# A decoder layer's MLP: the sums of w_down formed later, h's first reload moved, and the last product and final norm taken tile by tile

## The chip, the cores and the metric

The kernel runs on one core of one Trainium2 chip. The metric is the time of one execution on the device in microseconds (us), lower is better. All data is float32 and starts and ends in DRAM.

## The reference

One layer of a hybrid decoder, on 1024 tokens of width 1024, cut here to its steps:

```python
h = x
n = rms_norm(h, ln_mix_g)
ya = dilated_mixture(rope(q), rope(k), v) @ w_branch_a      # 12 heads of 64
yb = stick_breaking(qb, kb, vb) @ w_branch_b                # 8 heads of 64
h = h + (sigmoid(ga + b) * ya + sigmoid(gb + b) * yb) @ w_out
h = h + memory_cross_attn(rms_norm(h, ln_x_g), rms_norm(mem, ln_mem_g), ...)
u = conv3(rms_norm(h, ln_ffn_g) @ w_up) + conv_b            # 1024 -> 2 x 2816
h = h + (silu(u[:, :2816]) * u[:, 2816:]) @ w_down          # 2816 -> 1024
out = rms_norm(h, ln_f_g)
```

## The kernel before, in words

Every product in full precision is three TensorE matmuls (`mm3`, lines 98 to 101): both operands are split into a high and a low part by ACT (L82) and DVE (L83), and high x high, low x high and high x low are summed in PSUM. A matmul has 128 x 128 weights and 512 columns.

The program goes through these stages: the dilated attention and then the stick-breaking attention (`sb_unit`), with the projections of later heads between their units; the merge of both branches under their gates; `w_out`; cross attention; then the MLP, in two parts.

**w_up** has 22 rows g of 128 features for the gate half (ug) and the value half (uv). The products follow a Strassen-like scheme with seven products of half size in place of eight, so a row has sums of weights (`sum_weights`, on DVE) and sums of results. Each row is three functions: `up_start` (loads of the weights, the first product into bank pA), `up_middle` (three products into pA and pB, and pD for rows from the tenth on) and `up_end` (two products, then convolution, silu and the product of the halves). The driver calls `up_start(g)`, `up_end(g - 1)`, `up_middle(g)`. `add_into` copies a PSUM bank into half of ug or uv by ACT and adds a sum to it by an accumulating DMA on POOL's queue (L918): uv<-U of U4 for the upper half, uv<-U of U2 for the lower half. Then `up_end` reads uv by ACT (L966) and twice by DVE (L967, L968). The results go to DRAM (`r_d`) by DMAs on POOL's queue. ug and uv share two buffers (tag "hu"), so a row's uv follows the uv of the row before in the same place.

The first ten rows (`NEARLY`) begin with results that were made early and are read back from `er_d` and `e_d`.

**w_down** (`down`) also has seven products, each over 11 pairs of rows kg and four tiles of 128 tokens. `run(ps, i, first, also)` loads product i's left operand from `r_d` and its right one from w_down or from `sd_d`, splits them (`dh`, `dl`) and goes over the four tiles for every kg; `also` is a list of DMAs, one issued after each kg from the fourth on, by which h is read back from `h_d`. `into` adds the banks to h and, where `last` is given, forms the squares for the final norm. `out_half` scales four tiles of h and stores them.

**The sums of w_down** in `sd_d` are made by DMAs alone (`weight_sums`, L515): for each of 11 pairs kg, four `put` of 256 KB, DRAM to DRAM on SP's queue (L519), and three accumulating `add` on POOL's queue (L522), of 512, 256 and 256 KB. They alternate and each waits for the one ahead. `sum_step` takes one step: block b starts at step 3b and does an operation every second step. Before, it is called once per unit of the stick-breaking attention (`p >= NA`) and once per step of the merge. Puts and adds are kept where the program wrote them by `keep_in_program_order`.

Elsewhere the order on every engine is set by the compiler's scheduler, which simulates a timeline and takes what it thinks ready; so instructions can stand in another order than written. PSUM banks come from `bank`, SBUF tiles from pools with a fixed number of buffers per tag; a tile waits until the last reader of its buffer is done.

Of the kernel before, what the change touches and what calls it, by code (L numbers as in the profile page):

```python
# [7 lines left out]
F32 = mybir.dt.float32  # L8
F32R = mybir.dt.float32r
# [33 lines left out]
def hybrid_layer(ctx: ExitStack, tc: tile.TileContext, x, xT, mem, memT, w_in, w_v, w_br, w_out, w_xq, w_xk, w_xv, w_xo, w_up,  # L43
# [492 lines left out]
    def sum_step():  # L536
        n = sums_n[0]
        sums_n[0] += 1
        for b, ops in enumerate(sums):
            d = n - 3 * b  # L540
            if 0 <= d < 12 and d % 2 == 0:
                ops[d // 2]()

    for fn in proj_pair(0):
        fn()
# [2 lines left out]
    for p in range(NA + NS):  # L548
        units = [(dil_step, (8 * p + i,)) if p < NA else (sb_unit, (p, i)) for i in range(8)]
        if p == NA:  # L550
            units[CPOS:CPOS] = [(combine, (0,)), (combine, (1,))]
            units = [(dil_step, (8 * NA + i,)) for i in range(3)] + units
        gemms = [(fn, ()) for fn in proj_pair(p + 1)] if p + 1 < NA + NS else []
        ng = len(gates) if p == NA + NS - 1 else GATES[p]
        for _ in range(ng):
            gemms.append((gate, (gates.pop(0),)))
        nu, ngm = len(units), len(gemms)
        if p == NA + NS - 1:
            ngm = TAIL_MIX
        k = 0  # L560
        for u, (fn, a) in enumerate(units):
            while k < ngm and k * nu <= u * ngm:
                gemms[k][0](*gemms[k][1])
                k += 1
            fn(*a)
            if p >= NA:
                sum_step()
        while k < len(gemms):
            gemms[k][0](*gemms[k][1])
            k += 1  # L570
# [64 lines left out]
        yT.append((hi, lo))  # L635
    merged = [act2(), act2()]
    for m in range(NK):
        sum_step()
        gs = []
        for j in (m, 8 + m):  # L640
            g = ap.tile([P, T], F32, tag="kg", name="g", bufs=4)
            nc.sync.dma_start(g, ga_d[j])
            nc.scalar.activation(g, g, AF.Sigmoid, bias=vec[:, V_BG + j:V_BG + j + 1])
            gs.append(g)
        ws = []
        for _, wh, wl in wchunks(w_br[m], 768):
            ws += [(wh[:, c:c + P], wl[:, c:c + P]) for c in range(0, wh.shape[1], P)]
        for th in range(2):
            hs = slice(th * HT, (th + 1) * HT)
            pa = pp.tile([P, HT], F32, tag="mm", name="pa", bufs=3)  # L650
            pbr = pp.tile([P, HT], F32, tag="mm", name="pbr", bufs=3)
            for j in range(6):
                yh, yl = yT[j]
                mm3(pa if j < 2 else pbr, ws[j], (yh[:, hs], yl[:, hs]), j in (0, 2), j in (1, 5))
            ga, gb = gs[0][:, hs], gs[1][:, hs]
            nc.vector.tensor_tensor(ga, pa, ga, op=ALU.mult)
            nc.vector.tensor_tensor(gb, pbr, gb, op=ALU.mult)
            nc.vector.tensor_tensor(ga, ga, gb, op=ALU.add)
            hilo(merged[th][0][:, m], merged[th][1][:, m], ga)
# [274 lines left out]
        return res  # L934

    def up_middle(g, u):
        for n in ("ug", "uv"):
            nc.gpsimd.memset(u[n][:, 0:2], 0.0)
        if g < NEARLY:
            nc.sync.dma_start(u["ug"][:, 2:2 + HT], e_d[g])  # L940
        else:
            d = bank("mm", 3, "pD")
            product(d, u["l12"], R["21"], True)
            add_into(u["ug"][:, 2:2 + HT], d, u["p1"])
        s1, s2, s3, u["s4"] = sum_weights(u)
        product(u["A"], s2, R["t2"], False)
        u["U2"] = etile("U2")
        nc.scalar.activation(u["U2"], u["A"], AF.Copy)
        u["B"] = bank("tr", 2, "pB")
        product(u["B"], s3, R["t3"], True)  # L950
        product(u["A"], s1, R["t1"], False)
        u4 = etile("U4")
        nc.scalar.activation(u4, u["A"], AF.Copy)  # L953
        add_into(u["uv"][:, 2 + HT:2 + T], u["B"], u4)

    def up_end(g, u):
        product(u["A"], u["s4"], R["22"], False)
        nc.scalar.activation(u["ug"][:, 2 + HT:2 + T], u["A"], AF.Copy)
        product(u["B"], u["l22"], R["t4"], False)
        add_into(u["uv"][:, 2:2 + HT], u["B"], u["U2"])  # L960
        ys = []
        for n, cw, cb, sign in (("ug", vec, V_CB + g, 0), ("uv", ncw, V_CB + NF + g, 1)):
            c0 = 3 * g if sign else V_CW + 3 * g
            x_ = u[n]
            y = htile([P, T], "hy", "y")
            nc.scalar.activation(y, x_[:, 2:2 + T], AF.Identity, scale=cw[:, c0 + 2:c0 + 3], bias=vec[:, cb:cb + 1])  # L966
            nc.vector.scalar_tensor_tensor(y, x_[:, 1:1 + T], cw[:, c0 + 1:c0 + 2], y, op0=ALU.mult, op1=ALU.add)  # L967
            nc.vector.scalar_tensor_tensor(y, x_[:, 0:T], cw[:, c0:c0 + 1], y, op0=ALU.mult, op1=ALU.add)  # L968
            if not sign:
                nc.scalar.activation(y, y, AF.Silu)  # L970
            ys.append(y)
        a = ys[1]
        nc.vector.tensor_tensor(a, ys[0], a, op=ALU.mult)
        kg = g // 2
        if g % 2 == 0:
            nc.gpsimd.dma_start(r_d[kg, 0], a[:, :HT])
            evens["a"] = a
            return
        (r11, r12), (r21, r22) = halves(evens["a"]), halves(a)
        nc.gpsimd.dma_start(r_d[kg, 1], r21)  # L980
        nc.gpsimd.dma_start(r_d[kg, 2], r22)
        t = [mp.tile([P, HT + 8], F32, tag="ts", name="ts", bufs=3)[:, :HT] for _ in range(4)]
        nc.vector.tensor_tensor(t[0], r11, r12, op=ALU.subtract)
        nc.gpsimd.dma_start(r_d[kg, 4], t[0])
        nc.vector.scalar_tensor_tensor(t[1], r22, -1.0, t[0], op0=ALU.mult, op1=ALU.subtract)
        nc.gpsimd.dma_start(r_d[kg, 5], t[1])
        nc.vector.tensor_tensor(t[2], r22, r12, op=ALU.subtract)
        nc.gpsimd.dma_start(r_d[kg, 6], t[2])
        nc.vector.scalar_tensor_tensor(t[3], t[1], -1.0, r21, op0=ALU.mult, op1=ALU.subtract)
        nc.gpsimd.dma_start(r_d[kg, 3], t[3])  # L990

    def down():
# [10 lines left out]
            hs = slice(ch * HT, (ch + 1) * HT)  # L1003
            return [lambda t=t: nc.sync.dma_start(h[t][:, hs], h_d[t][:, hs]) for t in range(4 * th, 4 * th + 4)]

        def run(ps, i, first, also=()):
            for kg in range(KG):
                if i == 1 and kg < 6:
                    where = (bp, "wr", 2), (bp, "wh", 2), (bp, "wl", 2)
                else:  # L1010
                    where = (dn, "rl", 6), *(((dn, "dh", 2), (dn, "dl", 2)) if kg % 2 else ((mp, "mh", 2), (mp, "ml", 2)))
                raw, hi, lo = (pool.tile([P, 2, HT], d, tag=tag, name=n_, bufs=b) for (pool, tag, b), n_, d in
                               zip(where, ("rl", "dh", "dl"), (F32, F32R, F32R)))
                nc.sync.dma_start(raw[:, 0], r_d[kg, i - 1])
                nc.sync.dma_start(raw[:, 1], left[i - 1](kg))
                split_to(hi, lo, raw)
                if kg >= 3 and kg - 3 < len(also):
                    tc.keep_in_program_order(also[kg - 3]())
                for t in range(4):
                    ts_ = slice(t * P, (t + 1) * P)  # L1020
                    mm3(ps[t], (hi[:, 0, ts_], lo[:, 0, ts_]), (hi[:, 1], lo[:, 1]), first and kg == 0, kg == KG - 1,
                        skip_group_check=True)

        def into(ps, th, ch, op, last=None):
            for t in range(4):
                hs = h[4 * th + t][:, ch * HT:(ch + 1) * HT]
                nc.vector.tensor_tensor(hs, hs, ps[t], op=op)
                if last is not None:
                    square(4 * th + t, ch, etile("sq"), last)

        def out_half(th):
            fo = bp.tile([P, 4, D], F32, tag="a2h", name="fo", bufs=2)
            for t in range(4 * th, 4 * th + 4):
                ft, rs = fo[:, t % 4], ssq[t][:, 1:2]
                nc.vector.tensor_tensor(ft, h[t], gF, op=ALU.mult)
                nc.vector.tensor_scalar(ft[:, 0:HT], ft[:, 0:HT], rs, None, op0=ALU.mult)
                nc.scalar.activation(ft[:, HT:], ft[:, HT:], AF.Copy, scale=rs)
                for c in (0, HT):
                    nc.sync.dma_start(out[t * P:(t + 1) * P, c:c + HT], ft[:, c:c + HT])

        run(A, 1, True, load_h(0, 0))
        into(A, 0, 0, ALU.add)
# [9 lines left out]
        into(A, 1, 1, ALU.subtract, 0)  # L1052
        run(B, 4, False)
        into(B, 0, 1, ALU.subtract, 1)
        out_half(0)
        run(A, 3, False)
        into(A, 1, 0, ALU.add, 1)
        out_half(1)

    mem_prep()  # L1060
    w_out_half(0)
# [118 lines left out]
```

## Time and profile before

| | |
|---|---|
| runs | 1784.14, 1780.95, 1777.82 us, median 1780.95 |
| profiled execution | 1780.45 us, span in the trace 1778.6 us, mean granted clock 0.986 |
| PE / DVE / ACT / POOL busy | 95% / 63% / 49% / 18% |
| DMA moved | 273.01 MB, mean 153 GB/s |
| chain that ended last | PE 66%, issue 13%, DMA 10%, DVE 5% |

Read it so: TensorE (PE) is the engine to fill; the others matter where PE waits for them. PE's busy time counts matmuls that run slowly as well, so the granted clock has to be looked at beside it. The stages in time: dilated attention to about 365 us, stick-breaking attention to 765, merge, w_out, cross attention and the early parts of w_up to about 1145, w_up's rows to 1548, w_down to 1765, and the end.

### The profile page before, as it was taken

What the parts mean: (1) busy time and instruction counts of PE and PEld (TensorE: products, weight loads), DVE (VectorE), ACT (ScalarE), POOL (GpSimd) and SP (SyncE); (2) the same over time, 40 slices, a digit from 0 to 9 for tenths busy, and PEclk for the clock granted to TensorE, in tenths of its full rate; (3) what the DMA queues carried; (4) which work ended last, traced back from release to release, by engine and by line L of the source; (5) the groups of instructions that cost most, each with busy time, mean ns of one, the idle gap of its engine ahead of it and who ended that gap; (6) DMA issues with size and microseconds to landing.
All of it is one profiled execution on the core that took longest, in us unless ns stands there. A gap on an engine that the chain in (4) does not pass through costs nothing.

```text
span 1778.6 us, 23614 instructions
## 1 busy us (share of the span) xinstructions
PE 1693.4 (95%) x8598; PEld 1378.1 (77%) x8598; DVE 1113.0 (63%) x1737; ACT 871.0 (49%) x1495; POOL 326.9 (18%) x511
## 2 busy tenths in 40 slices
PE   7999999998999899999999989798999999989997
PEld 5977777878878787788888767576778888778885
DVE  3764654468757466575645666777777767655556
ACT  5344544466345445444534455454555555534344
POOL 0442333221112110001000102222222222200002
PEclk9999999999999999999999999899999999999999
DMA  7443333455774843566322325666755454677664
GB/s 305 113 123 92 107 83 84 134 134 145 200 140 118 159 113 95 180 181 249 131 95 72 130 83 178 206 165 184 211 148 157 136 136 125 188 259 231 214 191 140
DMA packets 106388, 273.01 MB, mean 153 GB/s; under 512 B 16096, under 2 KB 16352, under 8 KB 106272
## 3 DMA queue, kind: packets, MB, share of 16 engines
q1 hardware_dynamic: 66368, 166.68, 28.9%
q0 software_dynamic: 39904, 104.82, 24.1%
q8 instruction: 68, 1.11, 0.3%
q14 instruction: 48, 0.39, 0.1%
HBM read 188.77 MB, written 74.29 MB: 148 GB/s over the span
## 4 chain that ended last, share of the span: by engine, by line
PE 66%; issue 13%; DMA 10%; DVE 5%; ACT 3%; POOL 3%; SPq 0%; POOLq 0%; DVEq 0%; ACTq 0%
PE mm L99 4%; PE mm L101 4%; PE mm L100 4%; PE pA L99 3%; PE pA L100 3%; PE pA L101 3%; DMA sd_d<-in_w_down_dram 2%; DMA uv<-U 2%; PE mmt L99 2%; PE dA L100 2%; PE dA L101 2%; PE mmt L100 2%; PE mmt L101 2%; PE dA L99 2%; DMA xw<-xs 2%
## 5 line engine op out<-in xcount | busy, mean ns | idle before, releaser
L101 PE MATMUL mm<-a2h,wl 128*128 128x512 f32 x592 | 235.2, 398 | 0.0
L99 PE MATMUL mm<-a2h,wh 128*128 128x512 f32 x592 | 234.7, 396 | 0.0
L100 PE MATMUL mm<-a2l,wh 128*128 128x512 f32 x592 | 234.5, 396 | 0.0
L83 DVE TENSOR_TENSOR wl<-wr,wh 128x1024 fp32r<-128x1024 f32 (+1 forms) x119 | 145.3, 1222 | 95.0 <-ACT wh L82 92.1
L82 ACT ACTIVATE wh<-wr 128x1024 fp32r<-128x1024 f32 (+1 forms) x119 | 124.0, 1043 | 132.6 <-PE mmt L101 29.2
L83 DVE TENSOR_TENSOR dl<-rl,dh 128x1024 fp32r<-128x1024 f32 x77 | 94.1, 1224 | 85.0 <-ACT dh L82 81.5
L82 ACT ACTIVATE dh<-rl 128x1024 fp32r<-128x1024 f32 x77 | 81.2, 1058 | 114.6 <-PE dA L101 41.2
L101 PEld LDWEIGHTS mm<-a2h,wl 128*128 128x128 f32 x592 | 112.4, 190 | 22.2 <-issue 1.0
L100 PEld LDWEIGHTS mm<-a2l,wh 128*128 128x128 f32 x592 | 112.3, 190 | 22.3 <-issue 0.9
L99 PEld LDWEIGHTS mm<-a2h,wh 128*128 128x128 f32 x592 | 112.5, 190 | 22.0 <-issue 0.9
L493 DVE TENSOR_TENSOR_SCAN kp<-kp 128x128 f32<-128x128 f32 (+7 forms) x64 | 86.8, 1356 | 29.4 <-ACT kp L490 29.1
L99 PE MATMUL pA<-a2h,mh 128*128 128x512 f32 x176 | 70.5, 400 | 14.9 <-ACT U L953 14.9
L502 ACT ACTIVATE at<-tra 128x512 f32<-128x512 f32 (+3 forms) x96 | 43.3, 489 | 76.9 <-PE tra L500 59.6
L112 POOL TENSOR_TENSOR ss<-ss,neghalf 128x1 f32<-128x1 f32 x24 | 23.3, 995 | 307.6 <-DVE ss L597 305.7
L490 ACT ACTIVATE kp<-zz,zsc 128x512 f32<-128x512 f32 (+3 forms) x96 | 55.6, 583 | 49.3 <-DVE zz L489 44.5
L381 ACT ACTIVATE sp<-sp,nm 128x128 f32<-128x128 f32 (+1 forms) x96 | 42.3, 442 | 72.6 <-DVE nm L379 72.5
L100 PE MATMUL dA<-dl,dh 128*128 128x512 f32 x176 | 70.1, 398 | 3.5 <-DVE dl L83 3.5
L101 PE MATMUL dA<-dh,dl 128*128 128x512 f32 x176 | 70.0, 397 | 0.0
L101 PE MATMUL pA<-a2h,ml 128*128 128x512 f32 x176 | 69.3, 394 | 0.0
L100 PE MATMUL pA<-a2l,mh 128*128 128x512 f32 x176 | 69.3, 394 | 0.0
L99 PE MATMUL dA<-dh 128*128 128x512 f32 x176 | 62.1, 393 | 3.8 <-ACT dh L82 3.8
L491 ACT ACTIVATE gg<-zz,zsc 128x512 f32<-128x512 f32 (+3 forms) x96 | 55.7, 583 | 7.1 <-DVE gg L494 7.1
(352 smaller groups left out, 4587.4 us busy)
## 6 DMA issues: line engine op xcount, KB each, us to landing
rl<-r_d SPq DMA_DIRECT2D x77, 256.0 KB, 3.2
wr<-in_w_in_dram SPq DMA_DIRECT2D x37, 512.0 KB, 4.2
wr<-in_w_up_dram SPq DMA_DIRECT2D x32, 512.0 KB, 4.3
w<-in_w_up_dram SPq DMA_DIRECT2D x22, 512.0 KB, 3.7
uv<-U POOLq DMA_DIRECT2D x44, 256.0 KB, 4.7
r_d<-ts POOLq DMA_DIRECT2D x44, 256.0 KB, 4.8
rl<-sd_d SPq DMA_DIRECT2D x44, 256.0 KB, 3.6
r_d<-y POOLq DMA_DIRECT2D x33, 256.0 KB, 3.4
```

The costliest lines, as they stand in the source:

```text
L82: nc.scalar.activation(hi, raw, AF.Copy)
L83: nc.vector.tensor_tensor(lo, raw, f(hi), op=ALU.subtract)
L99: nc.tensor.matmul(ps, wh, rh, start=first, stop=False, **kw)
L100: nc.tensor.matmul(ps, wh, ro, start=False, stop=False, **kw)
L101: nc.tensor.matmul(ps, wo, rh, start=False, stop=last, **kw)
L112: nc.gpsimd.tensor_tensor(ss, ss, neghalf[:, :n], op=ALU.pow)
L381: nc.scalar.activation(sp[:, a, :n], sp[:, a, :n], AF.Exp, scale=0.125, bias=nm[:, a:a + 1], accum_out=ost[:, 130 + a:131 + a])
L490: nc.scalar.activation(kp[:, c0:c1], z[:, :n], AF.Sigmoid, scale=zsc[:, 1, i:i + 1])
L491: nc.scalar.activation(gg[:, c0:c1], z[:, :n], AF.Sigmoid, scale=zsc[:, 0, i:i + 1])
L493: nc.vector.tensor_tensor_scan(rev, rev, rev, 1.0, op0=ALU.mult, op1=ALU.bypass)
L502: nc.scalar.activation(s[:, :nb * P], tp[:, :nb * P], AF.Copy)
```

## The change

`sum_step` is called in `up_middle` and `up_end` of w_up for rows g >= 6, and no longer in the attention and the merge. A block starts every second step and its six operations follow each other step by step. So there is one add in row 6, two in row 7, three in each of the rows 8 to 16, two in row 17 and one in row 18 (33), and 44 puts in the same rows. In `run`, the DMAs of `also` are issued from the seventh kg on in place of the fourth, and the loading and splitting is a function `operands`. With `ends=4`, which the last product has, the operands of the last four kg are loaded first and then taken tile by tile. `out_half` becomes `out_tile`, called by `into` after each tile of the last update of a half of h.

```diff
     def sum_step():
         n = sums_n[0]
         sums_n[0] += 1
         for b, ops in enumerate(sums):
-            d = n - 3 * b
-            if 0 <= d < 12 and d % 2 == 0:
-                ops[d // 2]()
+            d = n - 2 * b
+            if 0 <= d < 6:
+                ops[d]()
...
             fn(*a)
-            if p >= NA:
-                sum_step()
...
     for m in range(NK):
-        sum_step()
         gs = []
...
     def up_middle(g, u):
+        if g >= 6:
+            sum_step()
         for n in ("ug", "uv"):
...
     def up_end(g, u):
+        if g >= 6:
+            sum_step()
         product(u["A"], u["s4"], R["22"], False)
...
-        def run(ps, i, first, also=()):
-            for kg in range(KG):
...
-                nc.sync.dma_start(raw[:, 0], r_d[kg, i - 1])
-                nc.sync.dma_start(raw[:, 1], left[i - 1](kg))
-                split_to(hi, lo, raw)
-                if kg >= 3 and kg - 3 < len(also):
-                    tc.keep_in_program_order(also[kg - 3]())
-                for t in range(4):
-                    ts_ = slice(t * P, (t + 1) * P)
-                    mm3(ps[t], ...
+        def operands(i, kg):
...
+            nc.sync.dma_start(raw[:, 0], r_d[kg, i - 1])
+            nc.sync.dma_start(raw[:, 1], left[i - 1](kg))
+            return split_to(hi, lo, raw)
+
+        def run(ps, i, first, also=(), ends=0):
+            def step(t, kg, hi, lo):
+                ts_ = slice(t * P, (t + 1) * P)
+                mm3(ps[t], (hi[:, 0, ts_], lo[:, 0, ts_]), (hi[:, 1], lo[:, 1]), first and kg == 0, kg == KG - 1,
+                    skip_group_check=True)
+
+            for kg in range(KG - ends):
+                w = operands(i, kg)
+                if kg >= 6 and kg - 6 < len(also):
+                    tc.keep_in_program_order(also[kg - 6]())
                 for t in range(4):
+                    step(t, kg, *w)
+            ws = [(kg, *operands(i, kg)) for kg in range(KG - ends, KG)]
+            for t in range(4 if ends else 0):
+                for w in ws:
+                    step(t, *w)
...
                 if last is not None:
                     square(4 * th + t, ch, etile("sq"), last)
+                if last:
+                    out_tile(4 * th + t)
...
-        def out_half(th):
-            fo = bp.tile([P, 4, D], F32, tag="a2h", name="fo", bufs=2)
-            for t in range(4 * th, 4 * th + 4):
...
+        def out_tile(t):
+            if t % 4 == 0:
+                fo[t // 4] = bp.tile([P, 4, D], F32, tag="a2h", name="fo", bufs=2)
...
         run(B, 4, False)
         into(B, 0, 1, ALU.subtract, 1)
-        out_half(0)
-        run(A, 3, False)
+        run(A, 3, False, ends=4)
         into(A, 1, 0, ALU.add, 1)
-        out_half(1)
```

How the change moves instructions, at three places.

POOL's order in w_up, one row. Before, from the first instruction of row 13 to its second accumulate into uv (U is U4 in the first uv<-U and U2 in the second):

```order
L938 MEMSET ug 128x2
L938 MEMSET uv 128x2
L918 DMA ug<-p_11794 128x512
L976 DMA r_d<-y 128x512
L984 DMA r_d<-ts 128x512
L918 DMA uv<-U_11906 128x512
L918 DMA uv<-U_11879 128x512
```

Now, the same row from its uv on, with the first instructions of the next:

```order
L937 MEMSET uv 128x2
L915 DMA uv<-U_11876 128x512
L522 DMA sd_d<-in_w_down_dram 128x512 x2
L977 DMA r_d<-y 128x512
L522 DMA sd_d<-in_w_down_dram 128x1024
L985 DMA r_d<-ts 128x512
L915 DMA uv<-U_11849 128x512
L937 MEMSET ug 128x2
L915 DMA ug<-p_11903 128x512
```

The three adds of the sums (L522) and the two stores of `r_d` now stand between the two accumulates into the same uv.

SP's order in the same rows, loads of w_up's weights (`wr`, and `w` for the second half). Before:

```order
L901 DMA w_12067<-in_w_up_dram 128x1024
L72 DMA wr<-in_w_up_dram 128x1024
L901 DMA w_12206<-in_w_up_dram 128x1024
L72 DMA wr<-in_w_up_dram 128x1024
L901 DMA w_12358<-in_w_up_dram 128x1024
```

Now, with the puts of the sums (L519):

```order
L898 DMA w_12044<-in_w_up_dram 128x1024
L519 DMA sd_d<-sd_d 128x512
L519 DMA sd_d<-in_w_down_dram 128x512 x2
L72 DMA wr<-in_w_up_dram 128x1024
L898 DMA w_12190<-in_w_up_dram 128x1024
L519 DMA sd_d<-sd_d 128x512
L72 DMA wr<-in_w_up_dram 128x1024
```

Puts now stand between the loads of two rows' weights, and a put of the kind sd_d<-sd_d waits for an add.

PE at the end of the last product, its last twelve matmuls; dA_13129 to dA_13132 are the banks of the four token tiles, a dh its operands of one kg. Before:

```order
L99 MATMUL dA_13129<-dh_14701 128x512
L100 MATMUL dA_13129<-dl_14702,dh_14701 128x512
L101 MATMUL dA_13129<-dh_14701,dl_14702 128x512
L99 MATMUL dA_13130<-dh_14701 128x512
L100 MATMUL dA_13130<-dl_14702,dh_14701 128x512
L101 MATMUL dA_13130<-dh_14701,dl_14702 128x512
L99 MATMUL dA_13131<-dh_14701 128x512
L100 MATMUL dA_13131<-dl_14702,dh_14701 128x512
L101 MATMUL dA_13131<-dh_14701,dl_14702 128x512
L99 MATMUL dA_13132<-dh_14701 128x512
L100 MATMUL dA_13132<-dl_14702,dh_14701 128x512
L101 MATMUL dA_13132<-dh_14701,dl_14702 128x512
```

Now, the last two matmuls of the third tile and the first six behind them:

```order
L100 MATMUL dA_13131<-dl_14666,dh_14665 128x512
L101 MATMUL dA_13131<-dh_14665,dl_14666 128x512
L99 MATMUL dA_13132<-dh_14644 128x512
L100 MATMUL dA_13132<-dl_14645,dh_14644 128x512
L101 MATMUL dA_13132<-dh_14644,dl_14645 128x512
L99 MATMUL dA_13132<-dh_14651 128x512
L100 MATMUL dA_13132<-dl_14652,dh_14651 128x512
L101 MATMUL dA_13132<-dh_14651,dl_14652 128x512
```

Behind these stand six more of the same bank, of the operands 14658 and 14665, and nothing else; the other three tiles are done before.

## Rows read from the trace of the kernel before

**Rows 1.** The page's first part: busy time, share of the span, instructions.

```profile
PE 1693.4 (95%) x8598; PEld 1378.1 (77%) x8598; DVE 1113.0 (63%) x1737; ACT 871.0 (49%) x1495; POOL 326.9 (18%) x511
```

**Rows 2.** Busy time by stretch of the span.

```profile
core 0: us, PE busy (x) PEld busy (x) DVE busy (x) ACT busy (x) POOL busy (x), PEclk, DMA share, GB/s
200.00:320.00 120.00, 119.72 (x698) 95.33 (x698) 63.83 (x158) 59.55 (x157) 39.88 (x58) 1.00 0.35 91
365.00:765.00 400.00, 388.80 (x2299) 315.74 (x2298) 258.89 (x469) 195.11 (x352) 56.93 (x85) 0.99 0.61 146
492.00:507.00 15.00, 14.97 (x83) 11.13 (x82) 7.51 (x12) 6.85 (x13) 2.76 (x4) 1.00 0.93 159
615.20:620.00 4.80, 4.76 (x15) 3.85 (x16) 2.14 (x3) 3.30 (x7) 0.00 (x0) 0.50 1.02 136
1276.00:1465.00 189.00, 187.48 (x813) 152.63 (x814) 142.51 (x148) 103.24 (x134) 47.12 (x86) 1.00 0.54 148
```

**Rows 3.** What PE waited for: us in total, times, longest us.

```profile
PE pA L99 <- ACT U L953: 14.9, 8, 3.2
PE avs L507 <- ACT at L502: 7.6, 2, 5.0
PE dA L99 <- ACT dh L82: 3.8, 2, 2.1
PE dA L100 <- DVE dl L83: 3.5, 3, 1.6
```

**Rows 4.** Timeline near 608 us: start, length, instruction, [idle before, its releaser].

```profile
608.21 0.81 POOL L522 DMA_DIRECT2D sd_d<-in_w_down_dram  x1 [9.79 <-DMA sd_d<-sd_d]
609.30 0.84 POOL L513 DMA_DIRECT2D yt_d<-ye  x1
614.91 0.28 ACT L502 ACTIVATE at<-tra 128x128 f32<-128x128 f32 x1 [9.94 <-DMA yt_d<-ye]
615.24 0.69 PE L507 MATMUL avs<-at,v 128*64 128x128 f32 x2 [4.96 <-ACT at L502]
```

**Rows 5.** Timeline of one w_up row, uv's instructions.

```profile
1421.57 1.28 DVE L968 SCALAR_TENSOR_TENSOR y<-uv,ncw,y 128x1024 f32<-128x1024 f32 x1
1423.77 0.60 ACT L917 ACTIVATE uv<-pB 128x512 f32<-128x512 f32 x1 [0.54 <-PE pB L101]
1427.27 0.89 POOL L918 DMA_DIRECT2D uv<-U  x1 [1.49 <-ACT U L953]
1432.87 0.87 POOL L918 DMA_DIRECT2D uv<-U  x1 [4.71 <-ACT uv L917]
1437.24 1.24 ACT L966 ACTIVATE y<-uv,vec,ncw 128x1024 f32<-128x1024 f32 x1 [0.93 <-DMA uv<-U]
1446.62 0.89 POOL L918 DMA_DIRECT2D uv<-U  x1
```

**Rows 6.** DMA issues by window: KB each, median us to landing.

```profile
sd_d<-in_w_down_dram POOLq DMA_DIRECT2D x1, 512.0 KB, 11.7
sd_d<-in_w_down_dram POOLq DMA_DIRECT2D x1, 512.0 KB, 14.2
sd_d<-in_w_down_dram POOLq DMA_DIRECT2D x1, 256.0 KB, 5.2
ga_d<-xr POOLq DMA_DIRECT2D x1, 512.0 KB, 11.3
uv<-U POOLq DMA_DIRECT2D x20, 256.0 KB, 4.3
out_dram<-fo SPq DMA_DIRECT2D x1, 256.0 KB, 2.9
```

**Rows 7.** Timeline of the end.

```profile
1763.60 1.37 DVE L1027 TENSOR_TENSOR h<-h,dA 128x512 f32<-128x512 f32 x2 [6.55 <-PE dA L101]
1765.21 0.39 PE L101 MATMUL dA<-dh,dl 128*128 128x512 f32 x1
1769.36 5.72 SPq L1039 DMA_DIRECT2D out_dram<-fo  x8
```

More of the change, by code (lines that the diff above doesn't have):

```diff
@@ L1004, in load_h @@
             return [lambda t=t: nc.sync.dma_start(h[t][:, hs], h_d[t][:, hs]) for t in range(4 * th, 4 * th + 4)]
-        def run(ps, i, first, also=()):
-            for kg in range(KG):
[L1008 to L1013, printed above, removed]
-                nc.sync.dma_start(raw[:, 0], r_d[kg, i - 1])
-                nc.sync.dma_start(raw[:, 1], left[i - 1](kg))
-                split_to(hi, lo, raw)
-                if kg >= 3 and kg - 3 < len(also):
-                    tc.keep_in_program_order(also[kg - 3]())
-                for t in range(4):
-                    ts_ = slice(t * P, (t + 1) * P)
-                    mm3(ps[t], (hi[:, 0, ts_], lo[:, 0, ts_]), (hi[:, 1], lo[:, 1]), first and kg == 0, kg == KG - 1,
-                        skip_group_check=True)
+        def operands(i, kg):
+            if i == 1 and kg < 6:
+                where = (bp, "wr", 2), (bp, "wh", 2), (bp, "wl", 2)
+            else:
+                where = (dn, "rl", 6), *(((dn, "dh", 2), (dn, "dl", 2)) if kg % 2 else ((mp, "mh", 2), (mp, "ml", 2)))
+            raw, hi, lo = (pool.tile([P, 2, HT], d, tag=tag, name=n_, bufs=b) for (pool, tag, b), n_, d in
+                           zip(where, ("rl", "dh", "dl"), (F32, F32R, F32R)))
+            nc.sync.dma_start(raw[:, 0], r_d[kg, i - 1])
+            nc.sync.dma_start(raw[:, 1], left[i - 1](kg))
+            return split_to(hi, lo, raw)
@@ L1029, in into @@
                     square(4 * th + t, ch, etile("sq"), last)
-        def out_half(th):
-            fo = bp.tile([P, 4, D], F32, tag="a2h", name="fo", bufs=2)
-            for t in range(4 * th, 4 * th + 4):
[L1034 to L1039, printed above, removed]
+                if last:
+                    out_tile(4 * th + t)
+        fo = {}
+        def out_tile(t):
+            if t % 4 == 0:
+                fo[t // 4] = bp.tile([P, 4, D], F32, tag="a2h", name="fo", bufs=2)
+            ft, rs = fo[t // 4][:, t % 4], ssq[t][:, 1:2]
+            nc.vector.tensor_tensor(ft, h[t], gF, op=ALU.mult)
+            nc.vector.tensor_scalar(ft[:, 0:HT], ft[:, 0:HT], rs, None, op0=ALU.mult)
+            nc.scalar.activation(ft[:, HT:], ft[:, HT:], AF.Copy, scale=rs)
+            for c in (0, HT):
+                nc.sync.dma_start(out[t * P:(t + 1) * P, c:c + HT], ft[:, c:c + HT])
         run(A, 1, True, load_h(0, 0))
```

## The prediction

> **What bounds the kernel now.** Page first: TensorE (PE) is busy for 1693.4 of 1778.6 us, 95%, and no other engine passes 63% [rows 1]. So time is won only where PE idles or runs slowly, and lost wherever a new wait reaches PE. The busy time by stage comes next [rows 2]: in the w_up rows from the tenth on (1276 to 1465) PE is busy 187.48 of 189.00 us at full clock while the DMA engines are 54% used; in the stick-breaking stage, which now carries all the sums, they are 61% used, against 35% in the dilated stage before it, which has none. The list of what PE waited for [rows 3] is short: 7.6 us for `at` in the stick-breaking stage, 14.9 for `U` over eight first uses of a bank, and 3.8 and 3.5 at starts of products. The timeline then shows three places.
>
> Place 1, the worst stall of the stick-breaking stage [rows 4]. GpSimd (POOL) stood 9.79 us at an add of the sums, because that add reads what a put (sd_d<-sd_d) had not yet written. Behind it in POOL's order stood the store of `ye`; ACT's `at`, which takes over a buffer of the same tag, waited 9.94 us for that store, and PE 4.96 for `at`. For the next 4.80 us PE's granted clock was 0.50, 1.2 in place of 2.4 GHz [rows 2].
>
> Place 2, one steady row of w_up [rows 5]. A row's first accumulate into uv (of U4) is issued at 1427.27 and the next row's at 1446.62: a period of 19.35 us, equal to the row's PE work, so PE sets it. The second one (U2) goes out at 1432.87, 5.60 later, after POOL had waited 4.71 for ACT. `y<-uv` starts at 1437.24, released by its landing: 9.97 after the row's first issue. Then uv must be read by ACT (1.24) and twice by DVE (1.28 each), refilled by ACT (0.60), and `U` copied (0.60), before the next U4 can go: 5.0 us, 5.4 with 0.1 us for each of four handovers. So 9.97 + 5.4 = 15.4 of 19.35 are taken, and U2 may land 4.0 us later than now before the ring of uv becomes longer than PE's row.
>
> Place 3, the end [rows 7]. PE's last matmul starts at 1765.21; DVE takes up h at 1763.60; the stores go out from 1769.36 for 5.72 us and one needs 2.9 [rows 6].
>
> **The change, part by part.** Sums leave the attention stages: 33 adds and 44 puts are moved, none removed. Gain there: the 4.96 us stall goes, and with it the slow clock, 4.80 us at half speed = 2.4 us of work: 7.4 us. What would be late next at that place is `at` itself, whose other inputs PE had written before. PE's other wait of that line (7.6 - 5.0 = 2.6 us) I leave in. Bounds: 0, should the store of `ye` be late for the bank's sake anyway, and 10, if that other stall goes too (2.6). I take 7.4, since POOL's waiting ends on a put that is no longer there.
>
> The end: in the last four groups of the last product, three of the four token tiles now finish 12 matmuls or more before the end. At one matmul in 0.23 us (189 us for 813 in the w_up rows, [rows 2]) that is 2.8 us. Their h add, square, norm, scaling and stores then lie beside the last tile's matmuls; behind PE stays one tile's chain. Now 13.4 us lie between the start of the last matmul and the end of the span (1778.6 - 1765.21). I take 3 us of gain, the PE time handed over; bounds 1 (the chain of one tile with its store of 2.9 is not shorter) and 6 (the whole of the 5.72 us of stores shrinks to the last tile's).
>
> h reloaded three groups later: the same loads; at the first product PE waits 3.8 and 3.5 us for its own operands [rows 3], whose loads lie in front of h's. I put it at 0; bounds 4 gained (half of those 7.3), 1 lost.
>
> What w_up takes on: from the seventh row, one, two and then three adds a row (nine rows with three), and up to four puts of 256 KB on SP's queue between the loads of the weights. The order of POOL (shown above) has them between the U4 accumulate and the U2 accumulate of the same uv. The issue costs little: 0.5 to 0.9 us each, POOL idles. The landing matters, because what stands behind a batch in this queue lands behind it: such batches landed 11.7 and 14.2 us after the issue of the 512 KB add, and a plain store issued behind one needed 11.3 [rows 6]. A 256 KB add on its own took 5.2, the normal uv<-U 4.3. So in a row: U4 at 0, the three adds issued by 2.0, the last landed at 13.7 to 16.2, U2 some 2 us (about half of its 4.3) behind that: 15.7 to 18.2 instead of 9.97. With the 5.4 us of the ring the row becomes 21.1 to 23.6 us, 1.8 to 4.3 more than PE's 19.35. I take 3.0, the middle, for the eight rows from the tenth to the seventeenth: 24 us. For the rows with fewer adds (7, 8, 18 and 19) and the ninth, where the adds stand ahead of both accumulates, 2 us, bounds 0 and 8.
>
> A second count gives the same sign. Bytes: 0.54 x 19.35 = 10.4 us of a row are DMA time today. The sums cost (0.61 - 0.35) x 400 / 11 = 9.5 us of full DMA time a block [rows 2], an estimate, since the two stages differ in other transfers also. A block a row makes 19.9 of 19.35: the sixteen engines would be full. In the stretch 492 to 507, with a batch in flight, they were at 0.93. In a full queue every load of weights, every store and every accumulate is later. Bounds of the whole: 0, if all is absorbed, and 8 x 5.5 + 8 = 52.
>
> Sum: 1780.45 (the profiled execution) - 7.4 - 3 + 0 + 24 + 2 = 1796.05, **1796 us**. The profiled execution lies 0.5 us below the median of the runs shown, 1780.95; that is nothing against the terms.
>
> **Rivals.**
> *A, absorbed (faster).* The DMA engines have 46% to spare in these rows, POOL waits 4.71 us before U2 anyway, and U2 may land 4.0 us later at no cost. The batches measured above ran beside stores and loads of another stage. It decides at the last add of a batch: if it lands within about 12 us of U4's issue (13.97 less U2's 2), the row stays at 19.35. Then only the gains remain: 1780.45 - 7.4 - 3 = 1770. Against it: both batches seen took longer. The Trainium skill, "DMA: Bandwidth & Descriptors", section "Anatomy of one DMA — SWDGE (gpsimd) path", fits one transfer as 2.0 us plus its bytes over 436 GB/s; by that a row's three adds, one behind the other, would take an estimated 3.2 + 2.6 + 2.6 = 8.4 us and this rival would come true. The trace disagrees so far: 5.2 us for the small add alone, 11.7 and 14.2 for batches.
> *B, a draw.* Rows of about 20.5 to 20.9 us, 1.2 to 1.5 more: 8 x 1.35 = 10.8 eat the 10.4 that is gained: 1779 to 1783.
> *C, saturated (much slower).* SP holds puts that wait for adds, and the loads of weights queue behind those puts; the adds in turn wait for puts. The row then follows two full DMA trips and not one; at 25 us, 5.5 more, with 8 for the edge rows: 1780.45 - 10.4 + 52 = 1822. For it: at place 1 an add did stand 9.79 us for a put. Against it: SP is a step ahead of the row.
> *That the change does not do what it says:* the stall at 615 could stay, with the store of `ye` behind other POOL work. The forecast would be 7 higher, inside the range.
>
> **How the numbers follow.** About 0.3% (5.3 us) is what a measurement of this kernel tells from no change: faster is below 1775.6, slower above 1786.3. Rival A 0.29, since one favourable number (a batch some 3 us shorter) is enough. B 0.20: the lower end of my own row estimate (+1.8) lies near it. Slower 0.51: the forecast 0.38 (1787 to 1812 alone), C 0.13. The range takes in A with the larger gain at the end (1780.45 - 7.4 - 6 = 1767) and the upper bound of the cost with small gains (1780.45 - 5 - 1 + 52 = 1826).
>
> **What would show it.** In the changed profile: no POOL wait on sd_d and no 5 us stall near 615, so w_out begins some 7 us earlier; rows ten to seventeen at 21 to 24 us, with PE waiting for `uv` or `U` by way of uv<-U, whose landing is then 10 us or more (median 4.3 now); DMA share in these rows near 0.9; the span after the last matmul about 3 us shorter. If rows stay at 19.35 while uv<-U lands late, the ring was sized wrongly; if uv<-U lands in 5 us, the batches were, and A holds. If PE waits for weights (`mh`, `wh`) and not for uv, it is C.

## The result, and the profile after

The change is slower: median 1833.81 us (1829.25 to 1835.44, four runs) against 1779.65 (four runs of the kernel before beside them). The ratio is 1.0296, 95% interval 1.0269 to 1.0324, so 54 us were lost where the prediction had 16. Its sign was right, its size was not: the time lies outside the range, which ended at 1826.

Where the time went, by stage, from the two profiled executions (a stage ends at the first matmul of the next, a row of w_up at its first accumulate into uv; rows are counted from 1):

| us | before | after | difference |
|---|---|---|---|
| dilated attention, to the first stick-breaking matmul | 357.3 | 358.4 | +1.1 |
| stick-breaking attention | 381.2 | 376.1 | -5.1 |
| merge to the first matmul of w_up | 410.6 | 410.9 | +0.3 |
| w_up to row 1 | 11.8 | 11.9 | +0.1 |
| rows 1 to 8 | 134.4 | 144.5 | +10.1 |
| rows 9 to 17 | 171.4 | 220.3 | +48.9 |
| row 18 to the first matmul of w_down | 63.9 | 64.8 | +0.9 |
| w_down | 234.5 | 233.8 | -0.7 |
| after the last matmul's start | 13.4 | 11.8 | -1.6 |

The gains come to 7.4 us, and w_up lost eight times that (the rounded rows add up to 54.0, the spans differ by 53.8). The busy time by stretch of the change, rows 1 to 8, rows 9 to 17, and rows 10 to 17 alone (which took 154.5 us before):

```profile
1157.30:1301.70 144.40, 126.66 (x516) 100.38 (x515) 101.76 (x108) 72.46 (x91) 42.33 (x77) 0.95 0.76 204
1301.70:1522.00 220.30, 179.87 (x734) 143.31 (x734) 127.62 (x134) 93.28 (x121) 63.37 (x101) 0.92 0.87 195
1324.30:1522.00 197.70, 163.14 (x662) 129.87 (x663) 115.88 (x122) 85.00 (x111) 58.65 (x92) 0.91 0.89 194
```

PE no longer fills these rows as it does in [rows 2]. What it waits for in rows 9 to 17, and in the attention (`avs`), by the waits of the change:

```profile
PE pB L99 <- ACT uv L914: 36.7, 5, 9.0
PE pA L99 <- ACT U L947: 2.8, 1, 2.8
PE pA L99 <- ACT wh L82: 0.7, 1, 0.7
PE avs L507 <- ACT at L502: 4.0, 1, 4.0
```

The bank pB is not free until ACT has copied it to uv; weights (`wh`) cost it 0.7 us. With one more wait of 0.2 us, PE's waits in rows 9 to 17 come to 40.4 us. The other 8.4 of the 48.9 us lost there are PE's own matmuls: they kept it busy for 179.87 us, where the kernel before took 171.50 for about as many:

```profile
1295.30:1466.80 171.50, 171.50 (x747) 139.92 (x746) 127.69 (x133) 94.19 (x123) 42.91 (x79) 1.00 0.54 148
```

The granted clock was 0.92 in place of 1.00. The prediction counted a slow clock at place 1 and none here. What these rows would take with these waits at full clock no run shows.

In the chain that ended last, the accumulate has grown from 2% to 8%:

```profile
DMA uv<-U 8%; PE mm L99 5%; PE mm L101 5%; PE mm L100 5%; DMA xw<-xs 2%; PE mmt L99 2%; PE mmt L100 2%; PE dA L100 2%; PE dA L101 2%; PE mmt L101 2%; PE pA L99 2%; PE dA L99 2%; PE pA L100 2%; PE pA L101 2%; PE dB L101 2%
```

Row 15 of the change in its timeline, to be read against [rows 5]:

```profile
1448.33 0.92 POOL L915 DMA_DIRECT2D uv<-U  x1
1448.89 2.89 POOL L522 DMA_DIRECT2D sd_d<-in_w_down_dram  x3
1450.51 1.85 POOL L991 DMA_DIRECT2D r_d<-ts  x1
1451.92 1.33 POOL L915 DMA_DIRECT2D uv<-U  x1
1468.95 1.24 ACT L967 ACTIVATE y<-uv,vec,ncw 128x1024 f32<-128x1024 f32 x1 [9.80 <-DMA uv<-U]
1470.28 1.28 DVE L968 SCALAR_TENSOR_TENSOR y<-uv,ncw,y 128x1024 f32<-128x1024 f32 x1 [12.71 <-ACT y L967]
1473.00 0.60 ACT L914 ACTIVATE uv<-pB 128x512 f32<-128x512 f32 x1 [2.81 <-DVE y L969]
1473.65 0.79 PE L99 MATMUL pB<-t4h,wh 128*128 128x512 f32 x1 [8.79 <-ACT uv L914]
1474.38 0.86 POOL L915 DMA_DIRECT2D uv<-U  x1 [1.20 <-ACT U L952]
```

U2's accumulate is issued at 1451.92, earlier in its row than in [rows 5] (3.6 against 5.6 us), yet `y<-uv` is released by its landing only at 1468.95, after ACT idled 9.80 and DVE 12.71 us. From there on the order is as before: two passes of DVE, ACT's copy, PE (8.79 us idle, then 0.79 us for a matmul in place of 0.40), the next row. The row took 26.1 us. All rows with three adds between the accumulates, by the issue and the landing of their DMAs in the trace, each in us from the row's first accumulate:

```
row            10    11    12    13    14    15    16    17   mean
last add    +14.0 +18.3 +11.1 +16.5 +14.0 +17.4 +11.3 +17.2   15.0
U2 lands    +18.3 +19.6 +13.5 +20.1 +16.6 +20.5 +13.7 +20.6   17.9
next row    +27.7 +25.1 +21.3 +25.6 +24.4 +26.1 +21.6 +26.1   24.7
before:
U2 lands    +11.3 +13.8  +9.7  +9.6 +11.0  +8.7  +9.9 +11.3   10.7
next row    +18.1 +20.0 +19.2 +19.0 +20.5 +18.2 +19.3 +20.1   19.3
```

Landing by landing, U2 comes 1.3 to 4.3 us behind the last add, and the next row follows U2 by 5.5 to 9.4 us.

### The profile page after: what moved, and what is told of

Same layout as the page of the kernel before. It is cut to its first block, busy times and chain, and to the rows that moved or that the text cites. A ratio compares the mean times of both kernels' runs of the same rounds, so it can differ in the third digit from the quotient of the medians.

```text
span 1832.4 us, 23607 instructions
## 1 busy us (share of the span) xinstructions
PE 1712.1 (93%) x8598; PEld 1391.5 (76%) x8598; DVE 1116.1 (61%) x1737; ACT 870.2 (47%) x1495; POOL 325.3 (18%) x511
## 4 chain that ended last, share of the span: by engine, by line
PE 62%; DMA 13%; issue 10%; DVE 7%; ACT 5%; POOL 3%; SPq 0%; POOLq 0%; DVEq 0%; ACTq 0%
DMA uv<-U 8%; PE mm L99 5%; PE mm L101 5%; PE mm L100 5%; DMA xw<-xs 2%; PE mmt L99 2%; PE mmt L100 2%; PE dA L100 2%; PE dA L101 2%; PE mmt L101 2%; PE pA L99 2%; PE dA L99 2%; PE pA L100 2%; PE pA L101 2%; PE dB L101 2%
## 5 line engine op out<-in xcount | busy, mean ns | idle before, releaser
L100 PE MATMUL mm<-a2l,wh 128*128 128x512 f32 x592 | 234.5, 396 | 0.0
L99 PE MATMUL pA<-a2h,mh 128*128 128x512 f32 x176 | 72.1, 410 | 20.5 <-ACT U L952 17.7
L968 DVE SCALAR_TENSOR_TENSOR y<-uv,ncw,y 128x1024 f32<-128x1024 f32 x22 | 28.2, 1284 | 96.9 <-ACT y L967 96.9
L99 PE MATMUL pB<-t4h,wh 128*128 128x512 f32 x88 | 39.8, 452 | 36.7 <-ACT uv L914 36.7
```

The source lines that it names most:

```text
L99: nc.tensor.matmul(ps, wh, rh, start=first, stop=False, **kw)
L100: nc.tensor.matmul(ps, wh, ro, start=False, stop=False, **kw)
```

## The experiments

Three theories stand against each other. **Q** (queue): U2's accumulate lands behind the adds that POOL issued before it, and the ring of uv waits. **D** (demand): the sums fill the sixteen DMA engines wherever they stand. **S** (the prediction's rival C) says that puts on SP's queue hold up the weights. Ratios are to the kernel before, run beside each on the same chip; they carry 95% intervals.

**1. The sums back in the attention; the other two edits stay.** `sum_step` is called where it was.

> The change without its first part: the sums are made in the attention and the merge, as before; the later reload of h and the tile-by-tile end stay. Theory (the loss is all in w_up): w_up is back at 381.6 us, the stall of 5.0 us near 615 is back, the end is 1.6 shorter and w_down 0.7 shorter, as in the trace of the change: about 1777.5 us, ratio to before 0.998 to 0.9995. Rival (the end or the reload costs something that the slow w_up hides): 1782 or more.

Measured: 1779.71 us, 0.9978 (0.9963 to 0.9993). w_up is 382.1 us, `avs` waits 8.5 us again (longest 5.4), the end takes 11.8. The loss is all in the moved sums.

**2. Only the sums moved.**

> Only the sums are moved. Theory: first product of w_up 3.8 us earlier, w_up 59.9 us longer, as in the trace of the change: 1779.65 - 3.8 + 59.9 = 1835.7 us. Rival (part of the loss comes from the other two parts): under 1825.

Measured: 1832.42 us, 1.0285 (1.0259 to 1.0311); w_up 440.6 us. As expected.

**3. Same sums, same rows, behind U2.**

```diff
     def up_end(g, u):
-        if g >= 6:
-            sum_step()
...
         add_into(u["uv"][:, 2:2 + HT], u["B"], u["U2"])
+        if g >= 6:
+            sum_step()
+            sum_step()
```

(and none in `up_middle`).

> The whole change, with both steps of the sums of a row called in up_end behind the accumulate of U2, so that POOL's order has the adds behind both accumulates into uv; same bytes in the same rows. Theory Q (queue: U2's accumulate lands behind the adds, and the ring of uv waits for it): uv<-U lands again about 10 us after the row's first issue, rows of 19.4 to 20.5 us, total 1775 to 1790 us. Rival D (the sixteen DMA engines are full, wherever the adds stand): rows stay at 23 to 26 us, total 1820 or more.

Measured: 1786.61 us, 1.0021 (1.0006 to 1.0036): nine tenths of the loss is gone with the same bytes in the same rows. Rows 9 to 17 take 182.9 us in place of 220.3. Rows 1 to 8 take 139.1 in place of 144.5; there PE's order is another as well, see run 5. Rows 10 to 17 of that run:

```profile
1315.20:1478.00 162.80, 156.84 (x675) 125.83 (x674) 115.60 (x122) 84.83 (x113) 58.71 (x95) 1.00 1.02 237
```

What is left of PE's wait for uv in rows 9 to 17:

```profile
PE pB L99 <- ACT uv L914: 3.3, 2, 2.7
```

And the accumulates in its DMA issues, with the median landing, some still late behind other traffic:

```profile
uv<-U POOLq DMA_DIRECT2D x17, 256.0 KB, 8.2
```

Here the DMA share is 1.02 at 237 GB/s, against 0.89 at 194 in the change. So D is no bound on the change. It is the likely reason for what is left, 162.8 us for eight rows, 20.4 a row and 1.0 over the 19.3 before; run 6 bears on it.

**4. Puts alone.** The adds are not issued, so the sums are not formed; the puts stay.

> The whole change with the 33 adds of the sums left out; the 44 puts stay on SP's queue (the sums are then not formed). Theory Q: rows of w_up back at 19.3 us, total 1833.8 - 59.9 + 1 = 1775 us. Rival S (puts between the loads of the weights make w_up late): rows over 21 us, total over 1795. Rival D (bytes): the puts are about two fifths of what the sums move, so some 24 us of the 59.9 stay: 1798.

Measured: 1785.02 us, 1.0015 (0.9997 to 1.0032). Rows 9 to 17 fall to 175.1 us, 3.7 over before. But the puts have no add to wait for here and go out sooner: 24 of the 44 in rows 1 to 8, where the change has 9. Rows 10 to 13 still have four puts each, as in the change, and take 79.4 us against 76.3 before and 99.6 in the change, so puts by themselves are out. Puts that wait for adds can't occur in this run; for them the waits of the change speak. SP's queue stood 153.0 us for adds there:

```profile
SPq L519 <- DMA sd_d<-in_w_down_dram: 153.0, 21, 24.3
```

Yet PE waited only 0.7 and 0.2 us for weights in rows 9 to 17. So S is out in the change.

The ratio is 1.0015 where theory Q's 1775 us would be 0.9974, and the reason stands in rows 1 to 8: 145.8 us with no add anywhere. The 24 puts may have a part in that; but rows 3 to 5 of the change, which have two puts and no add, took 55.3 us against 50.0 before. Something else had slowed them.

**5. t4 ahead of t2 again.** In rows 4 to 9 the scheduler of the change had moved the product pB<-t4 of a row behind pA<-t2 of the next. The two accumulates of row 4 in the timeline of the kernel before:

```profile
1209.80 0.88 POOL L918 DMA_DIRECT2D uv<-U  x1 [0.45 <-ACT uv L917]
1214.59 0.89 POOL L918 DMA_DIRECT2D uv<-U  x1 [1.98 <-DVE y L967]
```

And of the change:

```profile
1209.16 0.88 POOL L915 DMA_DIRECT2D uv<-U  x1 [0.72 <-ACT uv L914]
1218.09 0.88 POOL L915 DMA_DIRECT2D uv<-U  x1 [2.10 <-ACT uv L914]
```

U2 goes out 8.9 us into the row in place of 4.8, behind twelve more matmuls of 0.23 us and a copy. It lands at 12.3 us in place of 10.4, and the row takes 18.3 in place of 17.0. The edit pins the first matmul of t2, for 0 < g < 10, behind what PE was given before it:

```diff
-        nc.tensor.matmul(ps, wh, rh, start=first, stop=False, **kw)
+        m = nc.tensor.matmul(ps, wh, rh, start=first, stop=False, **kw)
+        if pin:
+            tc.keep_in_program_order(m)
...
-        product(u["A"], s2, R["t2"], False)
+        product(u["A"], s2, R["t2"], False, 0 < g < NEARLY)
```

> The whole change, with the product t2 of rows 2 to 10 pinned behind product t4 of the row before on PE, the order that the kernel before had there. Theory O (order): from the fourth row on the scheduler of the change put t4 behind t2, U2's accumulate goes out 3 to 4 us later in a row and the ring of uv takes 18 to 19 us where PE needs 17; pinned, the first nine rows (first accumulate of row 1 to that of row 9) take about 136 us in place of 144.4, total 1826, ratio to before about 1.025. Rival (those 10 us come from the first adds and their traffic): 143 us or more, total 1832 or more, ratio 1.029.

Measured: 1830.03 us, 1.0266 (1.0246 to 1.0286), and 140.9 us for the eight rows. Half a hit: of the 10 us some 3.6 are gone. Run 3, whose PE order in these rows is that of before, has 139.1, so the order is worth about 4 to 5 us. Most of it shows in rows 3 to 5, ahead of the first add: 55.3 us in the change, 51.7 here and 51.0 in run 3. What is left, about 5 us, is not split further. The pin also moved the swap on: from row 12 the scheduler now puts t4 behind the next row's t2, and rows 9 to 17 took 224.0 us.

**6. Spread and behind U2.** Run 3 with the pin of run 5, and a block of the sums every third step over rows 1 to 21.

> The change with the adds behind U2's accumulate, t4 pinned ahead of t2, and the sums spread over rows 1 to 21 (a block every third step, an operation every second: one or two adds a row in place of three). Theory Q with D as the rest of the cost (three adds a row fill the DMA engines, DMA share 1.02 with the adds behind U2 and 1.3 us a row lost): DMA share about 0.8, w_up 382 to 386 us, the attention 5 us shorter as in the change, the end 1.6 shorter: ratio to before 0.995 to 0.998. Rival (anything in POOL's queue in w_up delays the stores and reads of these rows): w_up over 390, ratio over 1.001.

Measured: 1780.01 us, 0.9988 (0.9974 to 1.0001). Rows 9 to 17 take 172.5 us, 1.1 over before: with fewer adds a row, behind U2, the cost there is gone. But rows 1 to 8 take 143.4 and w_up 391.7, so the rival holds for the first rows, whose DMA share rose to 0.89 from 0.65 before. The ratio lies between what the two said.

**7. Thin, but between the accumulates.** The change's places, with the same slower steps over rows 1 to 20.

> The change with the adds where it has them, between the two accumulates into uv, but with a block of the sums every third step and an operation every second step, over rows 1 to 20: one or two adds a row in place of three. Theory Q says that a row pays only when U2's accumulate lands more than 4 us later than before: with one or two adds it lands at about 8 to 13 us after the row's first issue, and from the ninth row's first accumulate to the eighteenth's it takes 171 to 185 us; the earlier rows pay for order and traffic as in the change: ratio to before 1.000 to 1.012. Rival (a cost for each add, 48.9 us for 30 adds): the same 33 adds cost the same 50 us, ratio 1.025 or more.

Measured: 1804.18 us, 1.0109 (1.0087 to 1.0131); rows 9 to 17 took 182.4 us, as theory Q had it. That is not in proportion to the adds: 18 of them in these rows cost 11.0 us, where the change's 24 cost 48.9. A threshold is seen row by row: of its rows 9 to 17, those where U2 landed 8.6 to 13.3 us after the first issue took 17.3 to 18.6 us; where it landed at 13.9 to 17.1 they took 19.7 to 22.8. Rows 1 to 8, with adds from the start, took 157.8 us, which the expectation did not price.

**8. U2 by DVE.** The whole change, and one line:

```diff
-        add_into(u["uv"][:, 2:2 + HT], u["B"], u["U2"])
+        nc.vector.tensor_tensor(u["uv"][:, 2:2 + HT], u["B"], u["U2"], op=ALU.add)
```

> The whole change, with U2 added to the lower half of uv by DVE straight from PSUM, in place of ACT's copy and POOL's accumulating DMA: nothing that y reads then lands behind the adds of a row, while the sums move the same bytes in the same rows; 256 KB of accumulate a row are gone. Theory Q: rows 10 to 17 take 19.3 to 20.5 us in place of 24.7, total 1775 to 1790 us, ratio to before 0.996 to 1.005. Rival D (DMA engines full): 23 us or more a row, ratio over 1.015.

Measured: 1786.13 us, 1.0040 (1.0018 to 1.0061). Most rows from the tenth on take 19.3 to 21.3 us with all sums in the change's places; two take 25.2 and 27.5. Rows 1 to 8 fall to 131.5. The edit also removes 256 KB of accumulate a row, which run 3 did not. In the two long rows PE waits for something new, the weights that S had named:

```profile
PE pD L99 <- ACT wh L82: 11.2, 3, 6.1
```

So with U2 out of the queue the next limit shows, at DMA share 0.94 (from 1312 to 1478 us), and it is worth about 14 us.

**9. The store of `ye` by ACT.** Run 1 with `nc.scalar.dma_start` in place of POOL's for yt_d.

> Sums where the kernel before has them, the new end and the later reload, and the store of ye (yt_d) issued by ACT and not by POOL, so that no add of the sums stands ahead of it. Theory: the stall of 5 us near 615 and its slow clock go without moving the sums: 5.5 us less than the run with the sums back, ratio to before about 0.995. Rival (ACT now waits for DVE's copy, or at waits for something else): ratio 0.998 or more.

Measured: 1776.53 us, 0.9966 (0.9949 to 0.9982). The time is near the expectation and its reason isn't: the stick-breaking attention took 385.8 us, no less than before. The stall at 615 is gone, and others are there, by that run's waits from 358 to 744 us:

```profile
PE tra L500 <- DVE gg L494: 4.7, 4, 3.8
PE avs L507 <- ACT at L502: 4.1, 2, 3.9
```

Its profile has the gain in rows 1 to 8 (129.4 us), which the edit does not touch. How much of this is the spread between executions stays open: the same stage, with the same order on PE, took 131.8 to 134.4 us in four other profiles.

**10. The tile-by-tile end alone.**

> Only the tile-by-tile end; sums and h's reload as before. Theory: the end after the last matmul 1.6 us shorter, the rest the same: ratio to before 0.998 to 0.9995. Rival (the later reload of h carries the gain of the run with the sums back, 0.9978): ratio 0.9995 to 1.001.

Measured: 1781.87 us, 0.9994 (0.9982 to 1.0006): the end is 11.8 us in its profile in place of 13.4, too little to be told from no change by time.

**11. The sums between the attention and w_up.** Run 1 with `sum_step` in the merge, w_out, the keys and queries of the cross attention and its softmax.

> The new end and the later reload, and the sums made between the attention and w_up: one step of them per step of the merge, of w_out, of the keys of the cross attention, of its queries and of its softmax, a block every third step. There the DMA engines are 25 to 61% used and nothing on POOL's queue is awaited by a ring. Theory: the attention is 5 to 6 us shorter as in the change, w_up is 378 to 382 us as before, the end 1.6 shorter: ratio to before 0.994 to 0.997. Rival (the puts on SP's queue hold up the loads of w_out's weights, whose splits PE waits for): the stages between are 5 us or more longer, ratio 0.998 or more.

Measured: 1826.19 us, 1.0231 (1.0203 to 1.0260), a clear miss. The stages between took 463.0 us in place of 410.6; the steps followed each other faster there than in the attention, and 60 of the 77 transfers went out between 800 and 980 us. That stretch:

```profile
800.00:980.00 180.00, 152.83 (x682) 123.97 (x681) 76.97 (x127) 61.95 (x102) 30.94 (x43) 0.91 0.87 216
```

And PE's longest waits from 736 to 1000 us:

```profile
PE pv L99 <- ACT wh L82: 14.9, 3, 6.5
PE mmt L99 <- ACT wh L82: 5.5, 2, 3.1
```

And the wait of SP's queue for adds in the whole of that run:

```profile
SPq L519 <- DMA sd_d<-in_w_down_dram: 83.5, 19, 9.4
```

Here the rival fits, the loads of weights on SP's queue behind puts that wait for adds. It is not all: PE's waits for weights in these stages are 24.2 us (1.1 before) of the 52.4 lost, and PE's busy time grew by 18.2 at a granted clock of 0.94 (0.98 before).

**12. The sums back, and U2 by DVE.** Run 1 with the line of run 8: the sums in the attention, the new end, the later reload, U2 by DVE.

> A version that may beat both: the sums where the kernel before has them, the new end and the later reload, and U2 added by DVE. Theory: in rows 1 to 9 the kernel before is also held by the ring of uv (U2 lands 10 to 12 us after the row's first issue and the next row begins 5 to 6.6 behind that, 16.8 us for about 16.4 us of matmuls); with DVE the first nine rows take about 128 in place of 134 us, the later ones 19.0: ratio to before 0.994 to 0.997. Rival (DVE, which is 75% busy in these rows, is late with its splits): ratio 0.998 or more.

Measured: 1768.42 us, 0.9938 (0.9919 to 0.9957), faster than both kernels. Rows 1 to 8 take 126.9 us (134.4 before); rows 9 to 17 take 171.5, as before, since PE sets them. Rows 1 to 8 (a stretch of 128 us about them) and rows 10 to 17:

```profile
1162.00:1290.00 128.00, 118.16 (x505) 93.95 (x504) 106.83 (x120) 67.78 (x82) 32.88 (x68) 1.00 0.63 184
1304.70:1459.40 154.70, 154.70 (x673) 126.11 (x672) 118.84 (x128) 82.24 (x104) 31.16 (x60) 1.00 0.44 130
```

The rival is out: DVE carries the additional work, and PE is not late. The ring held the first rows of the kernel before, which nobody had touched. A sign of it stood in [rows 3]: the 14.9 us that PE waited for `U` all lie in rows 1 to 8. They are 17.7 in the change, 23.5 in run 4 and 9.8 here. (This profile is shorter in w_down also, 229.8 us, which the edit doesn't explain.)

## Why the prediction was right or wrong

**The sign and the place: right.** PE-bound rows, a wait that reaches PE through the ring of uv, adds between the two accumulates: runs 1 and 2 place the loss there, and runs 3 and 8 remove nearly all of it with the sums in the same rows, run 3 with the same bytes. The forecast of 0.9 for the DMA share in these rows came true too (0.89). What failed is the size: the sum had 26 us for w_up, and 60.0 came.

**The row: mis-sized.** The step was "15.7 to 18.2 instead of 9.97. With the 5.4 us of the ring the row becomes 21.1 to 23.6". The last add landed at 15.0 on average (13.7 to 16.2 was said; 11.1 to 18.3 in the single rows), so the batch was read rightly from [rows 6]. U2 landed 2.9 us behind it, not 2, and the ring took 6.8 us behind U2, not 5.4. In rows 11, 13, 15 and 17 it took 5.5, as reckoned. In rows 12, 14 and 16 it is 7.8. There POOL has four stores of r_d, the first of which waits for DVE's product of the two halves, between ACT's copy of U and the next U4. In row 14, whose next U4 goes out at 1448.33:

```profile
1445.12 0.59 ACT L952 ACTIVATE U<-pA 128x512 f32<-128x512 f32 x1
1446.14 0.58 POOL L981 DMA_DIRECT2D r_d<-y  x1 [1.42 <-DVE y L974]
1447.79 0.54 POOL L989 DMA_DIRECT2D r_d<-ts  x1
```

In these three rows PE is never idle either, at a granted clock of 0.90 to 0.95, so the stores need not be the whole of it; in row 14:

```profile
1423.91:1448.33 24.42, 24.42 (x97) 19.49 (x96) 16.26 (x18) 11.46 (x16) 8.72 (x15) 0.90 0.88 198
```

In row 10, with 9.4, there are five such stores, and DVE does a split and two sums of weights between the steps that they wait for. 17.9 + 6.8 = 24.7, 5.4 over 19.3, where 3.0 was taken. Over eight rows that is 43 us for 24. So the term that failed is this one: the sum had counted the handovers of ACT and DVE and left out what POOL does in between, though the kernel before has such stores there too.

**The ninth row and the edge rows: too small.** Rows 7, 8, 9, 18 and 19 were put at 2 us together, bounds 0 and 8; they cost 9.1. Of this 5.6 are the ninth row's. The three adds issued in row 8 stand ahead of both its accumulates; U2 landed at 17.5 us and the row took 22.6 in place of 17.0.

**The first rows: put at nothing.** Rows 1 to 6 have no term in the sum, and they lost 7.3 us, 5.3 of them in rows 3 to 5, ahead of the first add. The swap of t4 and t2 in PE's order stood in the changed order, and nothing in the sum priced it; runs 3 and 5 put it at about 4 to 5 us, and the rest is not split. These rows had no slack: run 12 shows that the ring held them before.

**The gains.** The stall at 615 went, as said; "7.4" for it became 5.1 in this profile (4.4 to 8.5 over the nine profiles that have no sums in the attention). The other stall, which was left in at 2.66 us, grew to 3.96 in the change, by its timeline:

```profile
443.12 3.25 PE L507 MATMUL avs<-at,v 128*64 128x128 f32 x30 [3.96 <-ACT at L502]
```

The end gave 1.6 for 3. The timeline of the change there:

```profile
1817.39 1.28 DVE L1038 TENSOR_TENSOR h<-h,dA 128x512 f32<-128x512 f32 x2 [5.08 <-PE dA L101]
1820.63 0.39 PE L101 MATMUL dA<-dh,dl 128*128 128x512 f32 x1
1821.75 2.88 POOL L112 TENSOR_TENSOR ss<-ss,neghalf 128x1 f32<-128x1 f32 x3 [19.62 <-DVE ss L595]
1824.11 4.55 SPq L1054 DMA_DIRECT2D out_dram<-fo  x8
```

DVE starts 3.2 us before the last matmul (1.6 in [rows 7]), as forecast, but the first norm factor is taken by POOL only at 1821.75, behind DVE's other work, and the first store leaves 3.5 us after that matmul, against 4.2. The later reload changed w_down by -0.7, which no run separates from nothing.

**The rivals.** C had the size of a row (25 us; 24.7 measured) by luck and not the mechanism: its puts did wait for adds, but PE waited 0.7 and 0.2 us for weights in rows 9 to 17. PE does wait for weights in run 8 (11.2 us) and run 11. A's condition, the last add landed by 12 us, held in two of eight rows, 11.1 and 11.3, and even those took 21.3 and 21.6. The fit of the Trainium skill ("DMA: Bandwidth & Descriptors", "Anatomy of one DMA — SWDGE (gpsimd) path"), by which A would have come true, gives an estimated 3.2 us for a 512 KB transfer. The trace does not bear that out for these adds: the change's DMA issues in rows 10 to 17 have a median of 13.6:

```profile
uv<-U POOLq DMA_DIRECT2D x16, 256.0 KB, 6.8
sd_d<-in_w_down_dram POOLq DMA_DIRECT2D x16, 256.0 KB, 8.7
sd_d<-in_w_down_dram POOLq DMA_DIRECT2D x8, 512.0 KB, 13.6
```

The second count (19.9 us of DMA time a row) was right as a demand: run 3 has 1.02 of 20.4, which is 20.8.

## What to carry to other kernels

A transfer that a ring waits for lands behind the bulk that the same queue was given before it, so look at the order of issue on the queue before counting bytes: the same transfers cost 49 us in nine rows ahead of it and 11.5 behind it. Price the ring by walking it through every engine that it crosses, the issuing one too, and read the changed order for swaps far from the edit, since a scheduler may move work that nobody named. Where a ring is close to the bound, taking one link off the queue (here 0.7 us of DVE for an accumulate of 4.3) can be worth more than the edit under study.

## What was not expected of the hardware

The queue's order held for plain stores also: a store of r_d issued 0.5 us behind a batch of adds, at 1450.51, landed 16.1 us later, 0.9 behind the batch's last add. And beside a batch other queues were late too: a load of w_up's weights on SP's queue, issued at 1451.48, took 14.5 us in place of the 3.7 that is the median of such loads before; PE didn't wait for it, since it was a row ahead. Whether the batch held it up or the puts on SP's own queue, no run separates.
